# Gated linear attention on one core: the reference point of the log decays, one for each block of 128 tokens

## The chip, the cores and the metric

One core of a Trainium2 chip runs the whole kernel. The metric is the device time of one execution in microseconds (us), from repeated runs; the profile is one more execution, recorded instruction by instruction.

## The reference: what is computed

Two layers of an encoder on 256 tokens of 1024 channels, in float32. Each layer norms its input, projects it, feeds three mixers (a long convolution done as a Fourier product, a gated linear attention in both directions, a pooling mixer), merges them by gates, projects, and runs a gated MLP. The change is in the linear attention alone, which has 4 heads of 128 channels:

```python
def _gla_direction(q, k, v, log_a, include_diag):
    ...                                               # C = 64 tokens a chunk
    b = jnp.cumsum(log_a.reshape(B, N, C, H, DK), axis=2)
    b_last = b[:, :, -1]
    q_e = q * jnp.exp(b)
    k_e = k * jnp.exp(-b)
    scores = jnp.einsum('bnthd,bnshd->bnhts', q_e, k_e)
    ...                                               # triangular mask, product with v
    k_dec = k * jnp.exp(b_last[:, :, None] - b)
    U = jnp.einsum('bnshd,bnshe->bnhde', k_dec, v)
    decay = jnp.exp(b_last)
    ...                                               # state carried over the chunks
    o_inter = jnp.einsum('bnthd,bnhde->bnthe', q_e, S_prev)
```

Written out, a query at token t and a key at token s of one head meet with the factor exp(b_t - b_s), where b is the running sum of the log decays; the second direction runs from the last token to the first. Any common reference can be taken off both sums without changing the product.

## The kernel before

The 256 tokens are two blocks of 128. Almost all work is products of activations with weights that stream in from memory: SyncE loads a chunk of 128x2048, ScalarE (ACT, line 98) rounds it to a short float32 form, VectorE (DVE, line 103) subtracts to get the rest, and TensorE (PE, line 112, helper `mm`) multiplies three times for each pair (`mm3`: upper by upper, upper by lower, lower by upper). The main units (`two_ftiles`, `branch` and so on) are emitted one after the other; side work (`Side`, `start`, `tick`) is emitted between them a step at a time. Outside of stretches marked by `open_window` a list scheduler then sets the order on each engine; on the chip each engine takes its own list strictly in order. Tiles named `b` and `s` lie in SBUF (4096 and 2048 bytes a partition), `p` are the eight banks of PSUM.

The linear attention comes in three parts of a layer:

- `decay_gate(h)`, side work, four times: log decays of a head for both directions (z = 0, 1), two scans over the tokens (lines 663 and 665) which `rmask` restarts at each 64 tokens, then `e = exp(b)` and `en = exp(-b)`, each one ACTIVATE of 128x512, and two small copies (lines 672 and 673) of the exponentials at the chunk ends into `ebl`.
- `qk_post`: when queries and keys come from PE, they are multiplied into `eb` and `enb` (DVE line 106 for queries, 103 for keys).
- `gla_head(h)`, side work, four times: scores of a head, mask, product with `v`, norm, output gate, transposes. Since the sums restart every 64 tokens, a product over a block of 128 is right only inside each chunk of 64. The parts between two chunks are repaired: scaled copies of keys (`kx`) and queries (`q2`) are made by 6 ACTIVATEs and 6 DVE operations of 128x64, and for each block two matmuls of 64x64 (stationary 128x64, 64 moving columns) write over the wrong quarter of the block's scores:

```python
for t in range(2):
    for z in range(2):
        mm(pa[:, z, t, :], ke[:, z, s], qe[:, z, s], True, True)
    mm(pa[0:CH, 0, t, CH:], kx[:, 0, 0, cs(t)], qe[:, 0, cs(2 * t + 1)], True, True)
    mm(pa[CH:, 1, t, 0:CH], kx[:, 0, 1, cs(t)], qe[:, 1, cs(2 * t)], True, True)
```

These operands are plain float32, and each such matmul stands as two records in the trace (so 32 matmuls of 64x64 in the program are 64 records). Weight products run in the short form and are one record each.

Of the kernel before, what the change touches and what calls it, by code (L numbers as in the profile page):

```python
# [15 lines left out]
AF = mybir.ActivationFunctionType  # L16
ALU = mybir.AluOpType

P = 128
DEPTH = 2  # L20
L = 256
# [4 lines left out]
CH = 64  # L26
POOL_WINDOWS = (2, 4, 8, 16)
PAD = 8

# chunks of the weight stream, per layer  # L30
NCHUNK = 71

# columns of the packed per-channel vectors
V_HYC = 0            # 12 tiles x (w0, w1, w2, b)
V_FFC = 48           # 22 tiles x (w0, w1, w2, b)
V_GB = 136           # 2 dirs x 4 heads
V_PS = 148           # 4
V_FB = 152           # b1, fr1, b2, fr2 (64 rows, twice)
NVEC = 160
# [37 lines left out]
def trunk(ctx: ExitStack, tc: tile.TileContext, a: dict, out: bass.AP):  # L77
    nc = tc.nc
# [5 lines left out]
    sml = Slots(spool, "s", 9, 2048)  # L84
# [7 lines left out]
    ahead = {"chunks": 3, "reserve": 0, "at": 0, "quiet": False, "still": False}  # L92
# [4 lines left out]
    def act(o, i, func=AF.Copy, **kw):  # L97
        ins = nc.scalar.activation(o, i, func, **kw)  # L98
        if func in TABLED:
            tc.stamp_issue_order_token(ins.ins, TOKEN)  # L100
# [10 lines left out]
    def mm(o, w, x, start, stop):  # L111
        ins = nc.tensor.matmul(o, w, x, start=start, stop=stop).ins  # L112
        if not isinstance(ins, tuple):
            newest["pe"] = ins
# [12 lines left out]
    def open_window(*more):  # L127
        """From here on PE, DVE and ACT keep the order of emission; splits only where a chain leaves room."""
        e = mybir.EngineType
        window.enter_context(tc.manual_schedule(engines={e.PE, e.DVE, e.Activation, *more}))  # L130
        ahead["quiet"] = True
# [4 lines left out]

# [1 line left out]
    xs = [cpool.tile([P, DM], F32, name=f"x{t}") for t in range(2)]  # L138
# [5 lines left out]
    rmask = cpool.tile([P, L], F32, name="rmask")  # L144
# [18 lines left out]

# [1 line left out]
    order = []  # L165
# [56 lines left out]
    def split_half(lead=True):  # L222
        """One more half of a chunk is split; the upper parts run one half ahead."""
        if state["l"] >= 2 * len(order):
            return
        if state["h"] == state["l"]:
            split_upper()
        if lead and state["h"] == state["l"] + 1 and state["h"] // 2 in raws and len(big.free) >= ahead["reserve"] + 4:
            split_upper()
        split_lower()  # L230
# [5 lines left out]
    def weights(n, at, width):  # L236
        """Upper and lower part of columns of a chunk."""
        half, at = divmod(at, 1024)
        return wh[n][half][:, at:at + width], wl[n][half][:, at:at + width]
# [16 lines left out]
    def load_constants():  # L256
        nc.gpsimd.memset(rmask[:].rearrange("p (c s) -> p c s", s=CH)[:, :, 0:1], 0.0)
        nc.gpsimd.dma_start(zt[:], a["zt"])
        nc.gpsimd.dma_start(fw1[:], a["fw1"])
        nc.gpsimd.dma_start(fw2[:], a["fw2"])  # L260
        nc.gpsimd.dma_start(edges[:], bass.AP(a["edges"].tensor, a["edges"].offset, [[0, P], [1, 64]]))
        newest["pool"] = nc.gpsimd.dma_start(pmask_f[:], a["pmask"]).ins

# [1 line left out]
    sides = []  # L265
# [73 lines left out]

# [1 line left out]
    def rstd_of(ss, width, n=1):  # L341
# [22 lines left out]
    def rstd_mean(ss):  # L364
        """(mean + eps) ** -0.5 of a mean that lies in two parts."""
        r = cpool.tile([P, 1], F32, tag="rstd", bufs=4, name="rstd")
        e = cpool.tile([P, 1], F32, tag="mse", bufs=4, name="mse")
        tsc(e[:], ss[:, 0:1], ss[:, 1:2], EPS, ALU.add, ALU.add)
        nc.gpsimd.tensor_tensor(out=r[:], in0=e[:], in1=mhalf[:, 0:1], op=ALU.pow)  # L369
        return r  # L370
# [43 lines left out]

# [1 line left out]
    def filter_mlp(i, h2):  # L416
# [23 lines left out]

    # ---- the implicit filters, their spectra: even part on the cosines, odd part on the sines; even and odd times
    # apart, whose sum is the spectrum at f and whose difference that at 256 - f ----
    def load_dft(kf, n):
        """Upper and lower part; even or odd times; cosines, sines; 128 columns."""
        kf[n] = big.get([P, 2, 2, 2, P], F32R)
        with tc.issue_after(newest["pool"]):
            nc.gpsimd.dma_start(kf[n][:], a[n])
# [79 lines left out]

# [1 line left out]
    handles = {}  # L529
# [4 lines left out]
    def chunk_x_stationary(n, xt, t, o, half, lows_late=False):  # L534
        """Products of a chunk, 512 columns over half of the rows, with x stationary; lows_late takes lower parts last."""
        xth, xtl = xt[0][half], xt[1][half]
        s = slice(t * P, (t + 1) * P)
        todo = [(k, m) for k in range(4) for m in range(3)]
        if lows_late:
            todo.sort(key=lambda km: (km[0] // 2, (0, 2, 1)[km[1]]))  # L540
        for k, m in todo:
            h, l = weights(n, k * 512, 512)
            x = xtl if m == 2 else xth
            mm(o, x[:, k, s], l if m == 1 else h, half == 0 and (k, m) == todo[0], half == 1 and (k, m) == todo[-1])
# [22 lines left out]
    def layer(i, xt, chains):  # L567
# [8 lines left out]

        # -- value and output gate of the linear attention, token-major
        ahead.update(chunks=3, reserve=4)
# [12 lines left out]
        for at, (n, t) in enumerate(seq):  # L591
            drain(chains[t], alone=True)
            m, j = divmod(n, 2)
# [18 lines left out]

        # -- low rank of the decay gates: four groups of 32 rows, x w_h, x w_h, x w_l, x w_h, of which the first
        # two keep their upper part and the last its lower one; the second meets the lower part of the second factor
        nl = pos_of[("lr", i)]
# [22 lines left out]
        enb = [big.get([P, 2, 2, L]) for _ in range(2)]  # L638
        ebl = sml.get([P, 4, 2, 4])

# [6 lines left out]
        def decay_gate(h):  # L647
# [20 lines left out]
            yield  # L668
            act(e, en, AF.Exp)
            act(en, en, AF.Exp, scale=-1.0)  # L670
            ec = e.rearrange("p z (c s) -> p z c s", s=CH)
            nc.vector.tensor_copy(ebl[:, h, 0, :], ec[:, 0, :, CH - 1])
            nc.vector.tensor_copy(ebl[:, h, 1, :], ec[:, 1, :, 0])

# [13 lines left out]

        # -- Hyena: x1, v of the first and second half of the channels
        zv = big.get([P, 4, L])  # L690
# [132 lines left out]

        # -- queries and keys
        drain(f_dec, *gates_ready)
# [7 lines left out]

        # -- pooling
        pw = sml.get([P, 4, P])
# [69 lines left out]
        def gla_head(h):  # L905
            qe, ke = eb[h // 2][:, h % 2], enb[h // 2][:, h % 2]
            vh = slice(h * P, (h + 1) * P)
            cs = lambda c: slice(c * CH, (c + 1) * CH)
            e = lambda z, c: ebl[:, h, z, c:c + 1]
            kx = sml.get([P, 2, 2, P])  # L910
            q2 = sml.get([P, 2, P])
            sc = nc.vector.tensor_scalar_mul
            for z in range(2):
                for m in range(2):
                    act(kx[:, 0, z, cs(m)], ke[:, z, cs(2 * m + z)], scale=e(z, 2 * m + z))
            sc(kx[:, 1, 0, cs(0)], kx[:, 0, 0, cs(0)], e(0, 1))
            sc(kx[:, 1, 0, cs(1)], ke[:, 0, cs(1)], e(0, 1))
            sc(kx[:, 1, 1, cs(0)], ke[:, 1, cs(2)], e(1, 2))
            sc(kx[:, 1, 1, cs(1)], kx[:, 0, 1, cs(1)], e(1, 2))
            act(q2[:, 0, cs(0)], qe[:, 0, cs(2)])  # L920
            sc(q2[:, 0, cs(1)], qe[:, 0, cs(3)], e(0, 2))
            sc(q2[:, 1, cs(0)], qe[:, 1, cs(0)], e(1, 1))
            act(q2[:, 1, cs(1)], qe[:, 1, cs(1)])
            yield
# [3 lines left out]
            for t in range(2):  # L928
                s = slice(t * P, (t + 1) * P)
                for z in range(2):  # L930
                    mm(pa[:, z, t, :], ke[:, z, s], qe[:, z, s], True, True)
                mm(pa[0:CH, 0, t, CH:], kx[:, 0, 0, cs(t)], qe[:, 0, cs(2 * t + 1)], True, True)
                mm(pa[CH:, 1, t, 0:CH], kx[:, 0, 1, cs(t)], qe[:, 1, cs(2 * t)], True, True)
            for z in range(2):
                mm(pb[:, z, :], kx[:, 1, z, :], q2[:, z, :], True, True)
            yield
            sml.put(kx, q2)
            pm = sml.get([P, 4, P])
# [57 lines left out]

        # -- gates, branch projections, merge
        merged = []
# [61 lines left out]

        # -- output projection, post norm, residual, norm of the channel mixer
        ahead.update(chunks=6, reserve=2)
# [21 lines left out]

        # -- channel mixer
        NB = 4
# [184 lines left out]
def _constants():  # L1271
    """Arrays that depend on shapes alone."""
    t = np.linspace(0.0, 1.0, L, dtype=np.float32)[:, None]
# [130 lines left out]
```

## Time and profile before

| | |
|---|---|
| time of three runs, median (lowest to highest) | 907.86 us (907.23 to 908.74) |
| profiled execution, first to last instruction | 907.4 us |
| PE busy | 896.0 us, 99% of the span |
| PE weight loads busy | 836.9 us, 92% |
| DVE busy | 635.5 us, 70% |
| ACT busy | 500.2 us, 55% |
| GpSimd busy | 35.0 us, 4% |
| data moved | 164.61 MB, mean 181 GB/s |

The profiled execution has no time of its own beside its span; the median of the runs lies 0.46 us above that span. The ends of PE's records are modelled and successive records overlap, so what one matmul costs is read from the start of one row to the start of the next, not from its own duration.

### The profile page before, as it was taken

The numbers are of one execution on the slowest core, as the hardware profiler recorded it, in microseconds if no ns is written. First come the engines' busy times: TensorE is split into PE (matmuls) and PEld (weight loads), VectorE is DVE, ScalarE is ACT, GpSimd is POOL, SyncE is SP. The second block draws the span as 40 slices with busy tenths as digits, with TensorE's granted clock in tenths as the row PEclk, the third lists the DMA queues.
The fourth block names the chain that finished last, engine by engine and source line by source line (L and its number), as shares of the span: only waits on it lengthen the run. The fifth ranks groups of instructions, "written<-read, shape, count | busy, mean of one in ns | idle before, by whom it ended". The sixth has DMA issues, their size and how long they took to land.

```text
span 907.4 us, 15309 instructions
## 1 busy us (share of the span) xinstructions
PE 896.0 (99%) x6336; PEld 836.9 (92%) x6336; DVE 635.5 (70%) x934; ACT 500.2 (55%) x773; POOL 35.0 (4%) x80
## 2 busy tenths in 40 slices
PE   7999999999999999999999999999999999999997
PEld 6899999999988999998888999999999899999885
DVE  5899988666657798765288979775754967776612
ACT  6777656544446676545167744674542766554511
POOL 3000000100000000000010000000000000000000
PEclk9999999999999999999999999999999999999999
DMA  8863546446627436555439445264653583555601
GB/s 285 319 219 131 184 142 217 151 144 238 226 87 267 163 113 232 187 186 198 173 107 344 165 139 196 95 224 149 233 186 140 183 285 136 186 187 167 227 1 46
DMA packets 26020, 164.61 MB, mean 181 GB/s; under 512 B 3178, under 2 KB 3317, under 8 KB 8032
## 3 DMA queue, kind: packets, MB, share of 16 engines
q1 hardware_dynamic: 22464, 151.70, 47.2%
q0 software_dynamic: 3488, 11.95, 4.1%
q8 instruction: 49, 0.80, 0.3%
q14 instruction: 19, 0.16, 0.0%
HBM read 162.59 MB, written 1.05 MB: 180 GB/s over the span
## 4 chain that ended last, share of the span: by engine, by line
PE 97%; DMA 1%; DVE 1%; ACT 0%; issue 0%; SPq 0%; DVEq 0%; POOLq 0%; ACTq 0%
PE p L112 96%; DMA raw<-in_wts 1%; PE p L356 1%; PE p L1134 0%; DVE b L106 0%; DVE b L103 0%; PE p L738 0%; PE p L967 0%; ACT b L98 0%; SPq L151 0%; DVE x L106 0%; DVEq L1400 0%; ACT s L98 0%; POOLq L1400 0%; PE p L1217 0%
## 5 line engine op out<-in xcount | busy, mean ns | idle before, releaser
L112 PE MATMUL p<-b,b 128*128 128x256 f32 (+2 forms) x5958 | 858.4, 305 | 3.7 <-ACT b L98 2.4
L112 PEld LDWEIGHTS p<-b,b 128*128 128x128 f32 x5958 | 796.2, 191 | 54.1 <-ACT b L98 3.0
L103 DVE TENSOR_TENSOR b<-raw,b 128x1024 fp32r<-128x1024 f32 x286 | 343.0, 1217 | 126.0 <-ACT b L98 70.5
L98 ACT ACTIVATE b<-raw 128x1024 fp32r<-128x1024 f32 x288 | 290.8, 1045 | 196.5 <-PE p L112 163.6
L103 DVE TENSOR_TENSOR b<-p,b 128x512 f32<-128x512 f32 (+2 forms) x64 | 40.7, 653 | 59.8 <-ACT s L98 51.6
L98 ACT ACTIVATE b<-p 128x512 f32<-128x512 f32 (+3 forms) x78 | 43.5, 567 | 37.9 <-PE p L112 26.5
L98 ACT ACTIVATE s<-p 128x256 f32<-128x256 f32 (+3 forms) x50 | 20.3, 415 | 77.8 <-PE p L112 77.0
L106 DVE SCALAR_TENSOR_TENSOR s<-p,vec,s 128x255 f32<-128x255 f32 x104 | 49.4, 479 | 6.5 <-ACT s L98 5.5
L98 ACT ACTIVATE b<-b 128x512 f32<-128x512 f32 (+4 forms) x38 | 26.2, 692 | 24.1 <-DVE b L103 21.4
L98 ACT ACTIVATE s<-p,vec 128x256 f32<-128x256 f32 x52 | 28.7, 556 | 15.9 <-DVE s L106 13.0
L98 ACT ACTIVATE s<-s 128x512 f32<-128x512 f32 (+5 forms) x44 | 26.0, 594 | 14.2 <-DVE s L106 6.5
L103 DVE TENSOR_TENSOR b<-b,b 128x512 f32<-128x512 f32 (+4 forms) x34 | 26.6, 782 | 9.0 <-ACT b L98 8.6
L98 ACT ACTIVATE b<-s 128x512 fp32r<-128x512 f32 x38 | 23.6, 626 | 12.1 <-DVE s L103 12.0
L103 DVE TENSOR_TENSOR b<-s,b 128x512 fp32r<-128x512 f32 x38 | 25.9, 687 | 4.6 <-ACT b L98 4.6
L103 DVE TENSOR_TENSOR b<-b,p 128x512 f32<-128x512 f32 x24 | 16.4, 685 | 12.1 <-PE p L112 12.0
L112 PE MATMUL p<-b,s 128*64 128x64 f32 (+3 forms) x144 | 22.4, 286 | 0.0
L103 DVE TENSOR_TENSOR s<-s,p 128x512 f32<-128x512 f32 x22 | 15.0, 683 | 8.4 <-ACT s L98 8.0
L112 PEld LDWEIGHTS p<-b,s 128*128 128x128 f32 (+2 forms) x144 | 15.0, 166 | 5.7 <-issue 3.1
L106 DVE SCALAR_TENSOR_TENSOR b<-p,vec,b 128x255 f32<-128x255 f32 (+1 forms) x40 | 19.0, 480 | 1.7 <-ACT b L98 1.5
L103 DVE TENSOR_TENSOR s<-s,s 128x512 f32<-128x512 f32 (+2 forms) x24 | 15.7, 666 | 2.0 <-ACT s L98 2.0
L109 DVE TENSOR_SCALAR mse<-ssq 128x1 f32<-128x1 f32 (+1 forms) x24 | 4.7, 197 | 17.6 <-ACT s L98 13.7
L369 POOL TENSOR_TENSOR rstd<-mse,mhalf 128x1 f32<-128x1 f32 x16 | 8.8, 553 | 209.5 <-DVE mse L109 209.5
(96 smaller groups left out, 292.3 us busy)
## 6 DMA issues: line engine op xcount, KB each, us to landing
raw<-in_wts SPq DMA_DIRECT2D x140, 1024.0 KB, 4.9
b<-in_gains POOLq DMA_DIRECT2D x7, 512.0 KB, 6.7
raw<-in_wts SPq DMA_DIRECT2D x4, 512.0 KB, 8.1
b<-in_dft POOLq DMA_DIRECT2D x4, 512.0 KB, 5.3
x<-in_x SPq DMA_DIRECT2D x4, 256.0 KB, 4.8
b<-in_gw POOLq DMA_DIRECT2D x2, 512.0 KB, 5.6
b<-in_fw POOLq DMA_DIRECT2D x2, 512.0 KB, 6.4
b<-in_decay POOLq DMA_DIRECT2D x2, 512.0 KB, 7.4
```

The costliest lines, as they stand in the source:

```text
L98: ins = nc.scalar.activation(o, i, func, **kw)
L103: nc.vector.tensor_tensor(out=o, in0=x, in1=y, op=op)
L106: nc.vector.scalar_tensor_tensor(out=o, in0=x, scalar=s, in1=y, op0=op0, op1=op1)
L109: nc.vector.tensor_scalar(out=o, in0=x, scalar1=s1, scalar2=s2, op0=op0, op1=op1)
L112: ins = nc.tensor.matmul(o, w, x, start=start, stop=stop).ins
L356: nc.tensor.transpose(ps[k // 4][:, k % 4, :], h[:, k * P:(k + 1) * P], ident[:])
L369: nc.gpsimd.tensor_tensor(out=r[:], in0=e[:], in1=mhalf[:, 0:1], op=ALU.pow)
```

## The change

The scans restart every 128 tokens instead of every 64. Of the sum at each token the value at the middle of its block (token 63 of a block for the first direction, 64 for the second) is taken off inside the exponential, as a bias that differs by channel: so each 128x512 exponential becomes four of 128x128, one for each direction and block. The middle values and their negatives are two small DVE operations on four columns; two exponentials of the middle values and two of the block-end values are kept as the factors between the two blocks. With one reference for the whole block, the block's scores are right as they come from the 128x128 matmul; the 64x64 matmuls and the scaled copies for them are gone, and only the product between the blocks keeps scaled copies (`kq`), two ACTIVATEs and two DVE operations of 128x128 a head.

```diff
-        nc.gpsimd.memset(rmask[:].rearrange("p (c s) -> p c s", s=CH)[:, :, 0:1], 0.0)
+        nc.gpsimd.memset(rmask[:].rearrange("p (c s) -> p c s", s=P)[:, :, 0:1], 0.0)
...
-        ebl = sml.get([P, 4, 2, 4])
+        ebl = sml.get([P, 4, 3, 4])
...
-            act(e, en, AF.Exp)
-            act(en, en, AF.Exp, scale=-1.0)
-            ec = e.rearrange("p z (c s) -> p z c s", s=CH)
-            nc.vector.tensor_copy(ebl[:, h, 0, :], ec[:, 0, :, CH - 1])
-            nc.vector.tensor_copy(ebl[:, h, 1, :], ec[:, 1, :, 0])
+            at = lambda ap, o, *dims: bass.AP(ap.tensor, ap.offset + o, [list(ap.ap[0]), *map(list, dims)])
+            mid, neg, cross = (ebl[:, h, j, :] for j in range(3))
+            nc.vector.tensor_copy(at(mid, 0, (2, 2), (1, 2)), at(en, CH - 1, (L + 1, 2), (P, 2)))
+            nc.vector.tensor_scalar_mul(neg, mid, -1.0)
+            for z in range(2):
+                for b in range(2):
+                    s = slice(b * P, (b + 1) * P)
+                    act(e[:, z, s], en[:, z, s], AF.Exp, bias=neg[:, 2 * z + b:2 * z + b + 1])
+            for z in range(2):
+                for b in range(2):
+                    s = slice(b * P, (b + 1) * P)
+                    act(en[:, z, s], en[:, z, s], AF.Exp, scale=-1.0, bias=mid[:, 2 * z + b:2 * z + b + 1])
+            act(cross[:, 2:4], mid[:, 1:3], AF.Exp)
+            nc.vector.tensor_copy(cross[:, 0:2], at(e, P - 1, (L + 1, 2)))
...
-            kx = sml.get([P, 2, 2, P])
-            q2 = sml.get([P, 2, P])
-            sc = nc.vector.tensor_scalar_mul
+            kq = sml.get([P, 2, 2, P])
             for z in range(2):
-                for m in range(2):
-                    act(kx[:, 0, z, cs(m)], ke[:, z, cs(2 * m + z)], scale=e(z, 2 * m + z))
-            sc(kx[:, 1, 0, cs(0)], kx[:, 0, 0, cs(0)], e(0, 1))
-            sc(kx[:, 1, 0, cs(1)], ke[:, 0, cs(1)], e(0, 1))
-            sc(kx[:, 1, 1, cs(0)], ke[:, 1, cs(2)], e(1, 2))
-            sc(kx[:, 1, 1, cs(1)], kx[:, 0, 1, cs(1)], e(1, 2))
-            act(q2[:, 0, cs(0)], qe[:, 0, cs(2)])
-            sc(q2[:, 0, cs(1)], qe[:, 0, cs(3)], e(0, 2))
-            sc(q2[:, 1, cs(0)], qe[:, 1, cs(0)], e(1, 1))
-            act(q2[:, 1, cs(1)], qe[:, 1, cs(1)])
+                cross = lambda j: ebl[:, h, 2, 2 * j + z:2 * j + z + 1]
+                act(kq[:, 0, z, :], ke[:, z, z * P:(z + 1) * P], scale=cross(0))
+                nc.vector.tensor_scalar_mul(kq[:, 1, z, :], qe[:, z, (1 - z) * P:(2 - z) * P], cross(1))
...
-                mm(pa[0:CH, 0, t, CH:], kx[:, 0, 0, cs(t)], qe[:, 0, cs(2 * t + 1)], True, True)
-                mm(pa[CH:, 1, t, 0:CH], kx[:, 0, 1, cs(t)], qe[:, 1, cs(2 * t)], True, True)
             for z in range(2):
-                mm(pb[:, z, :], kx[:, 1, z, :], q2[:, z, :], True, True)
+                mm(pb[:, z, :], kq[:, 0, z, :], kq[:, 1, z, :], True, True)
```

PE's list at the fourth head of the first layer, before: `p_72` are the scores inside the blocks, `p_73` those between the blocks, `p_69` and `p_74` units of the gates with weights `b_147` to `b_150`.

```order
L112 MATMUL p_69_2062<-b_2_104,b_148_1830 128x256
L112 MATMUL p_72_2154<-b_48_435,b_50_437 128x128 x2
L112 MATMUL p_72_2154<-b_48_435,s_50_2096 64x64 x2
L112 MATMUL p_72_2154<-b_48_435,b_50_437 128x128 x2
L112 MATMUL p_72_2154<-b_48_435,s_50_2096 64x64 x2
L112 MATMUL p_73_2155<-s_51_2097,s_50_2096 128x128 x2
L112 MATMUL p_74_2166<-b_1_103,b_149_1877 128x256
```

The same place in the list of the changed kernel.

```order
L112 MATMUL p_69_2055<-b_2_104,b_148_1840 128x256
L112 MATMUL p_69_2055<-b_2_104,b_147_1839 128x256
L112 MATMUL p_69_2055<-b_4_106,b_147_1839 128x256
L112 MATMUL p_72_2138<-b_48_435,b_50_437 128x128 x4
L112 MATMUL p_73_2139<-s_47_2089 128x128 x2
L112 MATMUL p_74_2146<-b_1_103,b_149_1883 128x256
```

The four matmuls of 64x64 are gone and the six of 128x128 stand in one row; nothing has come in their place.

ACT's list at the decay gate of the first head in the first layer, before: `b_47` takes the exponential and `b_49` its inverse, `s_12`, `s_10` feed the filter spectra by `b_31`, `b_33`, `s_14` is the gate of the next head.

```order
L98 ACTIVATE s_14_730<-s_14_730 128x512
L98 ACTIVATE b_47_434<-b_49_436 128x512
L98 ACTIVATE s_19_824<-p_24_690,vec 128x256
L98 ACTIVATE b_31_323<-s_12_662 128x512
L98 ACTIVATE b_49_436<-b_49_436 128x512
L98 ACTIVATE b_33_325<-s_10_660 128x512
L98 ACTIVATE b_78_892<-raw_688 128x1024
```

The same place of the changed kernel; `s_7` holds the middle values.

```order
L98 ACTIVATE s_14_730<-s_14_730 128x512
L98 ACTIVATE s_19_832<-p_24_690,vec 128x256
L98 ACTIVATE b_31_323<-s_12_662 128x512
L98 ACTIVATE b_47_434<-b_49_436,s_7_438 128x128 x4
L98 ACTIVATE b_49_436<-b_49_436,s_7_438 128x128 x3
L98 ACTIVATE b_33_325<-s_10_660 128x512
L98 ACTIVATE b_49_436<-b_49_436,s_7_438 128x128
L98 ACTIVATE s_7_438<-s_7_438 128x2
L98 ACTIVATE b_78_916<-raw_688 128x1024
```

The first exponential has moved behind the work for `s_19` and `b_31`, and seven of the eight small exponentials now stand ahead of the split `b_33` that had one of 128x512 ahead of it.

## Rows read from the trace of the kernel before

**Rows 1.** The page: span, and busy time of each engine.

```profile
span 907.4 us, 15309 instructions
PE 896.0 (99%) x6336; PEld 836.9 (92%) x6336; DVE 635.5 (70%) x934; ACT 500.2 (55%) x773; POOL 35.0 (4%) x80
```

**Rows 2.** Waits of PE over the whole span: total us, times, longest.

```profile
PE p L112 <- ACT b L98: 2.4, 1, 2.4
PE p L112 <- DVE b L103: 1.3, 2, 1.1
```

**Rows 3.** Busy time by stretch: length, PE, PEld, DVE, ACT, POOL; clock, DMA.

```profile
0.00:20.00 20.00, 15.25 (x67) 12.72 (x67) 8.67 (x22) 11.43 (x28) 7.06 (x21) 0.91 0.87 278
...
60.00:100.00 40.00, 40.00 (x302) 37.18 (x301) 39.09 (x73) 30.23 (x51) 1.64 (x3) 1.00 0.43 153
...
163.00:200.00 37.00, 37.00 (x314) 36.00 (x311) 22.39 (x40) 17.48 (x41) 2.65 (x4) 1.00 0.37 134
```

**Rows 4.** Groups of PE by shape: all matmuls of 64x64.

```profile
L112 PE MATMUL p<-b,s 128*64 128x64 f32 x64 | 7.0, 246 | 0.0
```

**Rows 5.** PE in order of time at the fourth head: start, us, form.

```profile
180.53 0.34 PE L112 MATMUL p<-b,s 128*64 128x64 f32 x4
180.79 0.71 PE L112 MATMUL p<-b,b 128*128 128x128 f32 x4
181.43 0.34 PE L112 MATMUL p<-b,s 128*64 128x64 f32 x4
```

**Rows 6.** The same stretch in cuts of 10 ns, so single records stand apart.

```profile
180.10 0.39 PE L112 MATMUL p<-b,b 128*128 128x128 f32 x2
...
180.32 0.28 PE L112 MATMUL p<-b,b 128*128 128x128 f32 x1
...
181.01 0.39 PE L112 MATMUL p<-b,b 128*128 128x128 f32 x2
```

**Rows 7.** PE in order of time, score-by-value products of the third head.

```profile
176.22 1.06 PE L112 MATMUL p<-b,s 128*128 128x128 f32 x8
177.03 0.36 PE L112 MATMUL p<-b,b 128*128 128x256 f32 x1
```

**Rows 8.** PE in order of time, first 64x64 matmul of the program.

```profile
140.22 0.33 PE L112 MATMUL p<-b,s 128*64 128x64 f32 x2
140.48 0.62 PE L112 MATMUL p<-b,b 128*128 128x256 f32 x3
```

**Rows 9.** PE in order of time, last 64x64 matmuls of the program.

```profile
621.78 0.34 PE L112 MATMUL p<-b,s 128*64 128x64 f32 x4
```

**Rows 10.** Groups of ACT by shape.

```profile
L98 ACT ACTIVATE b<-b 128x512 f32<-128x512 f32 x16 | 9.9, 623 | 0.2
...
L98 ACT ACTIVATE s<-b,s 128x64 f32<-128x64 f32 x32 | 8.3, 337 | 0.5 <-DVE s L103 0.5
...
L98 ACT ACTIVATE b<-p,gcol 128x128 fp32r<-128x128 f32 x16 | 4.5, 389 | 2.6 <-PE p L1217 2.6
L98 ACT ACTIVATE s<-p 128x128 f32<-128x128 f32 x16 | 4.3, 276 | 3.0 <-PE p L112 3.0
```

**Rows 11.** Groups of DVE: one of six scalings, one of two copies.

```profile
L916 DVE TENSOR_SCALAR s<-s,s 128x64 f32<-128x64 f32 x8 | 2.0, 251 | 0.0
...
L673 DVE COPY s<-b 128x4 f32<-128x4 f32 x8 | 1.3, 168 | 0.0
```

**Rows 12.** ACT and DVE in order of time, decay gates of the first layer.

```profile
79.45 0.61 ACT L98 ACTIVATE b<-b 128x512 f32<-128x512 f32 x1
79.96 0.62 ACT L98 ACTIVATE b<-s 128x512 fp32r<-128x512 f32 x1
...
98.70 1.30 ACT L98 ACTIVATE b<-b 128x512 f32<-128x512 f32 x2
...
104.28 1.29 DVE L106 SCALAR_TENSOR_TENSOR b<-p,b 128x512 f32<-128x512 f32 x2
```

**Rows 13.** PE in order of time: the spectrum matmuls behind that split.

```profile
80.69 1.19 PE L112 MATMUL p<-b,b 128*128 128x512 f32 x7
```

More of the change, by code (lines that the diff above doesn't have):

```diff
@@ L907, in gla_head @@
             vh = slice(h * P, (h + 1) * P)
-            cs = lambda c: slice(c * CH, (c + 1) * CH)
-            e = lambda z, c: ebl[:, h, z, c:c + 1]
-            kx = sml.get([P, 2, 2, P])
-            q2 = sml.get([P, 2, P])
-            sc = nc.vector.tensor_scalar_mul
-            for z in range(2):
-                for m in range(2):
-                    act(kx[:, 0, z, cs(m)], ke[:, z, cs(2 * m + z)], scale=e(z, 2 * m + z))
-            sc(kx[:, 1, 0, cs(0)], kx[:, 0, 0, cs(0)], e(0, 1))
-            sc(kx[:, 1, 0, cs(1)], ke[:, 0, cs(1)], e(0, 1))
-            sc(kx[:, 1, 1, cs(0)], ke[:, 1, cs(2)], e(1, 2))
-            sc(kx[:, 1, 1, cs(1)], kx[:, 0, 1, cs(1)], e(1, 2))
-            act(q2[:, 0, cs(0)], qe[:, 0, cs(2)])
-            sc(q2[:, 0, cs(1)], qe[:, 0, cs(3)], e(0, 2))
-            sc(q2[:, 1, cs(0)], qe[:, 1, cs(0)], e(1, 1))
-            act(q2[:, 1, cs(1)], qe[:, 1, cs(1)])
+            kq = sml.get([P, 2, 2, P])
+            for z in range(2):
+                cross = lambda j: ebl[:, h, 2, 2 * j + z:2 * j + z + 1]
+                act(kq[:, 0, z, :], ke[:, z, z * P:(z + 1) * P], scale=cross(0))
+                nc.vector.tensor_scalar_mul(kq[:, 1, z, :], qe[:, z, (1 - z) * P:(2 - z) * P], cross(1))
             yield
@@ L931, in gla_head @@
                     mm(pa[:, z, t, :], ke[:, z, s], qe[:, z, s], True, True)
-                mm(pa[0:CH, 0, t, CH:], kx[:, 0, 0, cs(t)], qe[:, 0, cs(2 * t + 1)], True, True)
-                mm(pa[CH:, 1, t, 0:CH], kx[:, 0, 1, cs(t)], qe[:, 1, cs(2 * t)], True, True)
             for z in range(2):
-                mm(pb[:, z, :], kx[:, 1, z, :], q2[:, z, :], True, True)
+                mm(pb[:, z, :], kq[:, 0, z, :], kq[:, 1, z, :], True, True)
             yield
-            sml.put(kx, q2)
+            sml.put(kq)
             pm = sml.get([P, 4, P])
```

## Prediction

> **What bounds the kernel now.** I read the page first: PE is busy 896.0 of 907.4 us [rows 1]. A busy PE can still hide waits, so the waits come next: PE waited for ACT once, 2.4 us, and for DVE twice, 1.3 us in all [rows 2]. The table by stretch puts these at the start: the first 20 us hold 15.25 us of PE work, while both stretches of the middle that matter here, 60 to 100 and 163 to 200 us, are full to the last hundredth, at the granted clock of 1.00, that is at the 2.4 GHz level [rows 3]. So from 20 us on the end of the kernel is set by the sum of PE's intervals. Work taken off PE's list comes off the time one for one, as long as no other engine becomes late; work added to ACT or DVE costs nothing, as long as PE's operands and banks come in time.
>
> **What is removed on PE.** 32 matmuls of 64x64 go, 64 records with 7.0 us of busy time [rows 4]. That column isn't their price, since successive records overlap and the neighbours may be held up too. The price is read from starts. At the fourth head four records of 64x64 start at 180.53 and the next row at 180.79: 0.26 us for the group itself [rows 5]. The neighbours: 128x128 records ahead of the group start at 180.10 (two of them) and 180.32, so 0.22 / 2 = 0.11 us each; but from the last of them, 180.32, to the first 64x64 record at 180.53 it is 0.21 [rows 5, 6]. Behind the group the first 128x128 record starts at 180.79 and the second at 181.01: 0.22 instead of 0.11 [rows 5, 6]. So each side of a group costs 0.10 to 0.11 us more than a plain interval. One group is 0.26 + 0.10 + 0.10 = 0.46 us.
>
> Is the side cost really that of the 64x64 shape, not of these float32 products standing amid the short-form stream? The eight records of 128x128 at 176.22 are float32 too, follow other work and are followed by the stream at 177.03: 0.81 us for eight, 0.10 each, no side cost at either end [rows 7]. So it is the shape.
>
> Here a rule bears on how to count. The Trainium skill, TensorEngine Tiling (Array Packing), sections Key Properties and Theoretical Speedup, says that parts of 64 columns can run side by side, for up to twice the speed, and that a change of tiling mode drains TensorE. By its first half alone the removed matmuls would be cheap, down to half of their busy time, 3.5 us in all as an estimate; by its second half each group pays for entering and leaving. The trace agrees with both: it shows the sharing inside a group and the price at its sides.
>
> From rows, the sharing looks like this: the first group of the program has two records only, and from 140.22 to the next row at 140.48 it is 0.26 us as well, the same as for four [rows 8]. So the price goes by groups and not by matmuls. In the trace of the whole program I count 21 groups, 12 in the first layer and 9 in the second, of which 11 have four records and 10 have two (11 x 4 + 10 x 2 = 64), the first at 140.22 and the last at 621.78 [rows 8, 9]. 21 x 0.46 = 9.7 us. Rounding of the starts leaves about 0.01 us per group, so 9.4 to 10.0. Between the lists nothing takes their place on PE: the six 128x128 matmuls of a head are unchanged in number and shape, and in the list of the fourth head they stand together. The filter spectra move by some tens of rows in the first layer, with nothing added. The lists of SyncE and GpSimd keep their rows but for a memset of two columns instead of four, so no transfer moves past another; `gla_head` holds one `s` tile where it held two.
>
> **What is added and removed on ACT.** Per head, two exponentials of 128x512 at 623 ns go and eight of 128x128 come. The trace has no such operation from SBUF with a bias by channel; the nearest are 389 ns (a per-channel scale, from PSUM) and 276 ns (no per-channel operand) [rows 10]. So 2.2 to 3.1 us instead of 1.25, plus one tiny exponential, which I bound by 0 and 0.28. I take the upper end, since the 389 ns row also has a per-channel operand: at most +2.1 us per head, +1.0 at least. In `gla_head` six ACTIVATEs of 128x64 go, of which the four with a scale alone are 1.35 us (337 ns each; the two plain copies I leave out), and two of 128x128 come, 0.55 to 0.78 us: at least -0.6 to -0.8 us [rows 10]. Over the 8 heads of both layers ACT's total moves by +2 to +12 us on 500; it isn't near the bound as a whole. What counts is the stage of the decay gates.
>
> **What is added and removed on DVE.** Per head, two copies of four columns (168 ns) become two copies and one small product: +0.17 us; six scalings of 128x64 (251 ns, 1.5 us) become two of 128x128, which I bound by 0.25 and 0.50 each (one and two of the old): -0.5 to -1.0 us [rows 11]. DVE as a whole gets lighter, but the +0.17 us falls into 60 to 100 us, where it is busy 39.09 of 40 [rows 3].
>
> **The cover of the decay stage.** The longer chain of a head is: scan, copy, negative, four exponentials, four more. With the prices above it is 0.17 + 0.17 + 3.1 - 1.25 = 2.2 us longer than before. Who waits for it: the queries' product on DVE (line 106), behind which DVE's list and, through the PSUM bank it frees, PE's. In the first layer the last two exponentials start at 98.70 and are done at 100.00; the first query product starts at 104.28 [rows 12]. That leaves 4.3 us, more than the 2.2 us of one chain. If all four heads' extra ACT work ran up without being absorbed, it would be 4 x 2.1 = 8.4 us, against 40 - 30.23 = 9.8 us of idle ACT in the stretch [rows 3]: it just fits, so I cost it at nothing. If that cover is gone, the query products are late by 8.4 - 4.3 = 4.1 us.
>
> **Sum.** 907.4 - 9.7 = 897.7 us of span. The median of the runs shown is 0.46 us above the profiled span, so 898.2 us: 1.1% faster.
>
> **The rivals.**
>
> *The 64x64 work runs beside other work, and only part of its price comes back.* Then the sides stay, for instance since a float32 block has such an edge wherever the list puts it, and 21 x 0.26 = 5.5 us come off: 902.4 us. For it: groups of two and of four cost the same, so something does run side by side; and the list around the heads is rebuilt, so that other neighbours meet. Against it: the plain edges of the eight 128x128 records. Chance 0.06. It is the first half of the page's rule, that parts of 64 columns share the array, which would lead here.
>
> *The decay stage becomes late by part of its cover.* PE then waits up to 4.1 us in the first layer for banks or for spectra, and the time is 898.2 + 1.5 to 4.1, that is 899.7 to 902.3. For it: DVE has 0.9 us free in 40, and ACT would go from 30.23 to as much as 38.6. Against it: the same crowding costs PE nothing now. Chance 0.11.
>
> *Each head's exponentials hold up a split that PE needs at once.* This is the one on the other side. On ACT the split into `b_33` used to have one 128x512 exponential ahead of it and has seven of 128x128 in the new list. Such a split can be just in time: the one into `b_31` at 79.96 stands right behind an exponential (79.45) and ends at 80.58, and the spectrum matmuls that read it start at 80.69 [rows 12, 13]. If PE stood still for the extra work of every one of the 8 heads, at 1.0 to 2.1 us, that is 8 to 17 us, against 9.7 gained: it decides from 1.2 us per head, and at 2.1 the time would be 898.2 + 16.8 = 915. Against it: PE has gone through 8 such heads with no wait on record, because the list gives it weight products in between, and the first exponential was moved behind such a split. Chance 0.05; about 0.04 of no change lies between, with a wait of some 9 to 11 us.
>
> What I forecast has the rest, 0.74.
>
> **How the numbers follow.** A measurement of this kernel can tell about 0.2% from no change, 1.8 us. The forecast's own span is 9.4 to 10.0 us gained with up to 1.5 us lost to new waits, or a little more gained if the rebuilt list also drops some short stalls: 896.6 to 899.8. To leave out no more than 2 in 10 the range reaches on to 901.5, which takes in most of the second rival. Faster: 0.74 + 0.06 + 0.11 = 0.91; same 0.04; slower 0.05.
>
> **What would show each step right or wrong.** Right: the group of 64x64 matmuls is missing; in PE's order of time no interval of 0.2 us stands at a 128x128 record beside another shape in the heads; PE's busy time is near 896.0 - 9.7 = 886.3; PE's waits still sum to under 5 us, all at the start. The first rival would show as 0.2 us edges at the 128x128 runs. The second as waits of PE, or starved stretches of PE, between 60 and 140 us, with the query products of line 106 later relative to PE's work. The third as a new row of PE waiting for ACT, around the spectra. My prediction is wrong if PE's busy time falls by 9.7 but its idle time grows, since then the lists, and not the work, set the end; or if the starts that I read as a price were waits for scaled copies that something else would have filled.

## The result, and the profile after

| | before | after |
|---|---|---|
| median of four runs each, taken together (lowest to highest) | 907.56 us (907.23 to 908.74) | 901.64 us (900.64 to 902.33) |
| ratio, with 95% interval | | 0.9931 (0.9919 to 0.9943) |

The kernel is faster by 5.2 to 7.4 us, where 9.7 were forecast. The median is 0.14 us above the upper end of my range, inside the times of the second rival (899.7 to 902.3).

The page of the changed kernel, against [rows 1]:

```profile
span 898.9 us, 15183 instructions
PE 886.0 (99%) x6272; PEld 830.5 (92%) x6272; DVE 630.9 (70%) x910; ACT 505.8 (56%) x797; POOL 35.0 (4%) x80
```

PE is busy 886.0 us, where 886.3 were forecast. A part of that agreement is luck: the profiled run of before had the slower start (granted clock 0.91 in its first 20 us [rows 3], 1.00 here). Of the 10.0 us by which PE's busy time fell, 0.8 lie ahead of its 201st record, where both kernels have the same work; from there on it falls from 855.7 to 846.5 us, by 9.2. The waits of PE are the next thing to look at, against [rows 2]. Columns: total us, times, longest.

```profile
PE p L112 <- DVE b L103: 3.5, 3, 2.2
PE p L112 <- ACT b L98: 1.4, 1, 1.4
PE p L112 <- DVE rmask L246: 1.2, 1, 1.2
PE p L112 <- DMA b<-in_il: 0.5, 1, 0.5
```

Two of these are new: one of 2.2 us for DVE's line 103 and one of 0.5 us for a DMA. The wait for `rmask`, a mask made at the start, stands in both kernels; [rows 2] leave it out. The table by stretch says where; columns as in [rows 3].

```profile
0.00:20.00 20.00, 16.13 (x74) 13.04 (x74) 10.63 (x26) 13.38 (x31) 7.06 (x21) 1.00 0.86 281
60.00:100.00 40.00, 40.00 (x308) 38.03 (x308) 37.92 (x75) 31.39 (x66) 1.60 (x3) 1.00 0.33 119
100.00:140.00 40.00, 39.53 (x320) 38.85 (x320) 33.94 (x56) 24.11 (x41) 2.13 (x9) 1.00 0.48 164
140.00:163.00 23.00, 20.84 (x176) 20.64 (x175) 20.99 (x35) 15.14 (x28) 0.72 (x1) 1.00 0.69 236
```

The stretch with the decay gates, 60 to 100 us, is still full. PE stands still 0.47 us between 100 and 140 and 2.16 us between 140 and 163, at a granted clock of 1.00. The chain of waits leads back from the second hole (start, us, what):

```profile
113.49 9.00 DMA b<-in_il
...
122.54 13.96 PE p L112 x114
...
143.21 0.61 DVE b L103
```

PE's last link is the inverse transform of the convolution. All links from its end at 136.5 us to 143.82 are DVE's, one operation behind the other. DVE in order of time shows what it did there (the first row, a query product, is read further down):

```profile
106.70 0.68 DVE L106 SCALAR_TENSOR_TENSOR b<-p,b 128x512 f32<-128x512 f32 x1
...
137.23 0.68 DVE L103 TENSOR_TENSOR b<-p,b 128x512 f32<-128x512 f32 x1
...
139.06 0.47 DVE L923 TENSOR_SCALAR s<-b,s 128x128 f32<-128x128 f32 x2
139.45 2.35 DVE L103 TENSOR_TENSOR b<-raw,b 128x1024 fp32r<-128x1024 f32 x2
141.72 0.70 DVE L103 TENSOR_TENSOR b<-b 128x532 f32<-128x532 f32 x1
...
143.13 0.68 DVE L103 TENSOR_TENSOR b<-b,b 128x512 fp32r<-128x512 f32 x1
```

At 137.23 the second half of the convolution's output is multiplied (in `hyena`, `tt(zv...)`). Its lower split, which PE waits for, starts at 143.13. In between DVE works without a gap, on two splits of weights, on pooling steps, on the new scalings `kq` (line 923) and on a few more. That is 5.9 us from the multiplication to the split, but it isn't new. DVE at the same place before:

```profile
134.83 0.68 DVE L103 TENSOR_TENSOR b<-p,b 128x512 f32<-128x512 f32 x1
...
137.31 2.35 DVE L103 TENSOR_TENSOR b<-raw,b 128x1024 fp32r<-128x1024 f32 x2
...
140.92 0.69 DVE L103 TENSOR_TENSOR b<-b,b 128x512 fp32r<-128x512 f32 x1
```

There it took 6.1 us, with the same two splits of weights in between, and PE had no wait. PE in order of time has both holes of the changed kernel (the last three rows, the fourth head, are read further down):

```profile
122.54 14.42 PE L112 MATMUL p<-b,b 128*128 128x256 f32 x118 [0.47 <-DMA b<-in_il]
136.80 0.88 PE L112 MATMUL p<-s,s 128*128 128x256 f32 x6
137.52 2.61 PE L112 MATMUL p<-b,b 128*128 128x256 f32 x21
...
143.86 2.41 PE L112 MATMUL p<-b,b 128*128 128x256 f32 x18 [2.16 <-DVE b L103]
...
176.77 0.94 PE L112 MATMUL p<-b,b 128*128 128x128 f32 x7
177.55 0.61 PE L112 MATMUL p<-s 128*128 128x128 f32 x4
177.91 6.00 PE L112 MATMUL p<-b,b 128*128 128x256 f32 x48
```

PE goes on at 143.86, 0.73 us behind the start of that split. And PE before:

```profile
134.40 0.88 PE L112 MATMUL p<-s,s 128*128 128x256 f32 x6
135.12 5.17 PE L112 MATMUL p<-b,b 128*128 128x256 f32 x42
```

The six records of a pooling product (`p<-s,s`) start in both kernels 0.43 us ahead of DVE's multiplication. Before, 42 records and then the heads' follow them and cover DVE's stretch; now it is 21, and then 14 more up to the hole. The other work is not gone: the first of the six is PE's 899th record before and its 929th now, so 30 more records stand ahead of it.

Why does the output stand so late in PE's list? ACT in order of time, in the changed kernel (the first row, the last exponentials of the fourth head, is for later):

```profile
104.87 0.68 ACT L98 ACTIVATE b<-b,s 128x128 f32<-128x128 f32 x2
...
123.30 0.61 ACT L98 ACTIVATE b<-s 128x512 fp32r<-128x512 f32 x1
123.93 1.28 ACT L98 ACT_TABLE_LOAD   x1
126.32 1.06 ACT L98 ACTIVATE b<-b 128x1024 f32<-128x1024 f32 x1 [1.10 <-PE p L112]
127.28 0.58 ACT L98 ACTIVATE b<-p 128x512 f32<-128x512 f32 x1
127.76 0.62 ACT L98 ACTIVATE b<-s 128x512 fp32r<-128x512 f32 x1
```

And the same place before:

```profile
122.60 1.14 ACT L98 ACTIVATE b<-s 128x512 fp32r<-128x512 f32 x2
123.75 1.28 ACT L98 ACT_TABLE_LOAD   x1
```

Before, both last splits of the convolution's spectrum (`b<-s`, 128x512) stood ahead of the table load for the gate's sigmoid. In the changed kernel only one does; the other stands behind the load, the sigmoid (which itself waits for PE) and a copy, and starts 4.46 us after the first. The theory which the experiments had to test: the inverse transform's operands come late by this list, so the scheduler puts other work of PE ahead of its end, and too little is left behind it to cover the 6 us that DVE takes. PE never stands still for the late split itself: it has no wait near 128 us, where the split runs. The hole at 122.54 lies ahead of the split in time, and this theory doesn't account for it.

Runs of one kernel differ by up to 4 us, the longer ones mostly at a lower mean granted clock (in one kernel below 897.87 us at 0.999 and 900.90 at 0.994), so the fastest runs stand beside the medians.

### The profile page after: what moved, and what is told of

Its sections match the earlier page's. It is cut to its first block, busy times and chain, and to the rows that moved or that the text cites. A ratio compares the mean times of both kernels' runs of the same rounds, so it can differ in the third digit from the quotient of the medians.

```text
span 898.9 us, 15183 instructions
## 1 busy us (share of the span) xinstructions
PE 886.0 (99%) x6272; PEld 830.5 (92%) x6272; DVE 630.9 (70%) x910; ACT 505.8 (56%) x797; POOL 35.0 (4%) x80
## 4 chain that ended last, share of the span: by engine, by line
PE 96%; DMA 2%; DVE 2%; issue 0%; ACT 0%; SPq 0%; DVEq 0%; POOLq 0%; ACTq 0%
PE p L112 94%; DMA b<-in_il 1%; DVE b L103 1%; DMA raw<-in_wts 1%; PE p L356 1%; PE p L1132 0%; DVE b L106 0%; PE p L749 0%; PE p L965 0%; ACT b L98 0%; SPq L151 0%; DVE s L923 0%; DVE x L106 0%; DVEq L1398 0%; ACT s L98 0%
## 5 line engine op out<-in xcount | busy, mean ns | idle before, releaser
L98 ACT ACTIVATE s<-s 128x512 f32<-128x512 f32 (+6 forms) x52 | 27.7, 532 | 13.4 <-DVE s L106 8.2
L98 ACT ACTIVATE b<-b 128x512 fp32r<-128x512 f32 (+3 forms) x22 | 16.3, 742 | 24.8 <-DVE b L103 23.6
L98 ACT ACTIVATE b<-b,s 128x128 f32<-128x128 f32 x64 | 20.5, 391 | 1.0 <-DVE s L674 0.9
L112 PE MATMUL p<-b,s 128*128 128x128 f32 (+1 forms) x80 | 15.7, 315 | 0.0
```

## The experiments

The first four kernels ran together, with 17 runs of the kernel before: median 907.68 us, fastest 906.50. The last three ran together with 11 runs of it: median 906.68, fastest 906.32. The changed kernel was timed apart from both, with the four runs of before in the first table; against the kernel before of its own round each, it gained 5.9 us by the medians and 6.6 by the fastest runs.

The last column leaves the start out. It is read from the traces: the time from the start of PE's 201st record (at 42.6 to 46.0 us; all kernels have the same records up to there) to the end of PE's last one. Before it is 855.7 us, and in the changed kernel 849.1: 6.6 us less.

| kernel | median us | fastest | ratio to before (95%) | PE from its 201st record, us |
|---|---|---|---|---|
| before without 64x64 matmuls | 897.37 | 896.99 | 0.9891 (0.9873 to 0.9908) | 846.0 |
| before with eight exponentials a head | 908.08 | 906.27 | 0.9996 (0.9984 to 1.0008) | 855.1 |
| before, 64x64 matmuls grouped | 904.50 | 903.00 | 0.9960 (0.9945 to 0.9975) | 852.3 |
| after, sigmoid behind the split | 900.18 | 898.48 | 0.9912 (0.9897 to 0.9927) | 847.4 |
| after with two exponentials | 897.76 | 897.29 | 0.9894 (0.9877 to 0.9911) | 846.4 |
| before with the new heads | 898.32 | 897.23 | 0.9897 (0.9879 to 0.9914) | 846.3 |
| after, two edits of order | 899.15 | 897.87 | 0.9906 (0.9890 to 0.9923) | 846.7 |

**The price of the 64x64 matmuls, alone.** The kernel before without them; all scaled copies are still made.

```diff
-                mm(pa[0:CH, 0, t, CH:], kx[:, 0, 0, cs(t)], qe[:, 0, cs(2 * t + 1)], True, True)
-                mm(pa[CH:, 1, t, 0:CH], kx[:, 0, 1, cs(t)], qe[:, 1, cs(2 * t)], True, True)
```

> The kernel before, with the 32 matmuls of 64x64 left out and nothing else changed (the scaled copies are still made; the scores between the two 64-token chunks of a block are not repaired, so the output is not the reference's). Theory: the price of the 64x64 groups is 0.46 us each and all of it is on the path, so 9.7 us come off the time before (907.6): 897.9, and the wait of about 2.3 us that the changed kernel has near 141 us is missing, because ACT's list keeps the last spectral split ahead of the table load. Rival 1: the side costs stay or the matmuls partly ran beside other work: 5.5 us or less come off, 902.1 or more. Rival 2: the 64x64 matmuls were filling a wait for the second half of the convolution's output, so without them PE waits there whatever ACT's list: about 901.6, as the changed kernel.

Measured: 10.3 us less by the medians, 9.5 by the fastest runs and 9.7 by the last column, against the 9.7 of the sum. On the page PE is busy 885.2 us. All waits of PE:

```profile
PE p L112 <- ACT b L98: 1.4, 1, 1.4
PE p L112 <- DVE rmask L246: 1.2, 1, 1.2
PE p L112 <- DVE b L103: 1.2, 1, 1.2
```

All these waits lie in the first 20 us. So the price was right, it lay on the path in full, and the 64x64 matmuls had not been filling a wait.

**Does the price go by groups?** The kernel before with the four 64x64 matmuls of a head written behind its six of 128x128, which leaves 11 groups instead of 21.

```diff
             for z in range(2):
                 mm(pb[:, z, :], kx[:, 1, z, :], q2[:, z, :], True, True)
+            for t in range(2):
+                mm(pa[0:CH, 0, t, CH:], kx[:, 0, 0, cs(t)], qe[:, 0, cs(2 * t + 1)], True, True)
+                mm(pa[CH:, 1, t, 0:CH], kx[:, 0, 1, cs(t)], qe[:, 1, cs(2 * t)], True, True)
```

> The kernel before, with a head's four 64x64 matmuls written after its six of 128x128, so that PE's list has 11 groups of them instead of 21 (five of four, three of three, three of one). Theory of a price by groups: entering and leaving cost 0.20 us a group and the groups' own time is 0.26 us for up to two matmuls and 0.52 for three or four, so 3 x 0.46 + 8 x 0.72 = 7.1 instead of 9.7 us: about 2.5 us less than before (905.1). Rival, a price by matmul: no change.

Measured: 3.2 us less by the medians, 3.5 by the fastest runs, 3.4 by the last column, for the same 64 records. The interval of the times, 2.3 to 5.0 us, would hold my expectation of 2.5 as well as 4.6 for ten groups at 0.46. The trace decides. One group of four matmuls:

```profile
176.81 0.45 PE L112 MATMUL p<-b,s 128*64 128x64 f32 x8
177.19 0.98 PE L112 MATMUL p<-b,b 128*128 128x256 f32 x6
```

It takes 0.38 us from start to start, where I had expected 0.52; one or two matmuls take 0.26. The 11 groups of the trace (five of four matmuls, of which one takes 0.65, three of three at 0.38, three of one) sum to 4.1 us, and with 0.20 us at the sides of each to 6.3, against 9.7: 3.4 us less, as measured. So most of the price goes by groups, and a larger group costs a little more.

**The longer exponentials, alone.** The kernel before with eight exponentials of 128x128 a head, whose bias is a column of zeros.

```diff
-            act(e, en, AF.Exp)
+            for z in range(2):
+                for b in range(2):
+                    s = slice(b * P, (b + 1) * P)
+                    act(e[:, z, s], en[:, z, s], AF.Exp, bias=zero[:, 2 * z + b:2 * z + b + 1])
```

(The inverse likewise.)

> The kernel before, with the two exponentials of a head of 128x512 split into eight of 128x128 with a bias column of zeros; the 64x64 matmuls stay. Theory: the longer exponentials are covered, so the time stays within 1 us of the time before (907.6), with no new wait of PE. Rival: the crowded stage of the decay gates alone makes the filter's spectra or the convolution late, and it costs 2 to 4 us: 909.6 to 911.6.

Measured: no difference. Their group:

```profile
L98 ACT ACTIVATE b<-b,zero 128x128 f32<-128x128 f32 x64 | 20.8, 394 | 0.0
```

One costs 394 ns, and the crowded stage covers it. ACT's list at the convolution has, as before, both spectral splits ahead of the table load (120.64 and 121.79 us).

**The sigmoid held back.** The changed kernel; the gate's sigmoid may issue on ACT only behind the last spectral split.

```diff
-                split(yh[b][:, 1, :], yl[b][:, 1, :], p2[:])
+                newest["hy"] = nc.scalar.activation(yh[b][:, 1, :], p2[:], AF.Copy).ins
+                tt(yl[b][:, 1, :], p2[:], f32(yh[b][:, 1, :]), ALU.subtract)
...
+            with tc.issue_after(newest["hy"]):
-            act(gt[:], sg[:], AF.Sigmoid)
+                act(gt[:], sg[:], AF.Sigmoid)
```

> The changed kernel, with the sigmoid of the output gate in ACT's list held behind the last spectral split of the convolution, so that this split no longer waits for the table load, the sigmoid of 128x1024 and a bank copy. Theory: this misplaced split made the inverse transform late and PE used up its other work early; with it in place the wait near 141 us (2.3 us) goes, and with luck the one at 122 us (0.6 us): 898.7 to 899.3 against 901.6 of the changed kernel. Rival: the lateness comes from the crowded VectorE or from the late landing of the inverse transform's matrix, so that PE still waits about 2 us near there: 901 to 902.

Measured: 900.18 us, above what I expected. Against the kernel before of its round it gains 7.5 us (8.0 by the fastest runs), where the changed kernel gained 5.9 (6.6). The intervals of the two ratios overlap, so the times alone don't tell the two kernels apart; by the last column the edit gives back 1.7 us (849.1 to 847.4). PE in order of time, around both holes:

```profile
123.71 13.21 PE L112 MATMUL p<-b,b 128*128 128x256 f32 x108 [0.35 <-DMA b<-in_il]
...
137.48 3.80 PE L112 MATMUL p<-b,b 128*128 128x256 f32 x31
...
143.44 2.78 PE L112 MATMUL p<-b,b 128*128 128x256 f32 x21 [0.58 <-DVE b L103]
```

The wait for DVE falls from 2.16 to 0.58 us: the place of that one split caused most of it. PE's list shows how: ten of the records that stood ahead of the pooling product are back behind it (31 instead of 21, and 108 instead of 118 ahead). The wait for `in_il` stays, so this split didn't cause it.

**DVE's order as well.** The kernel above, with DVE's splits of weight chunks held behind the second split of the convolution's output.

```diff
+            with tc.issue_after(newest["hy2"]) if "hy2" in newest else ExitStack():
-            tt(wl[n][half][:], raws[n][:, half * 1024:(half + 1) * 1024], f32(wh[n][half][:]), ALU.subtract)
+                tt(wl[n][half][:], raws[n][:, half * 1024:(half + 1) * 1024], f32(wh[n][half][:]), ALU.subtract)
```

(`hy2` is the lower split of the second half in `hyena`.)

> The changed kernel with two edits of order: the gate's sigmoid on ACT is held behind the last spectral split, and DVE's lower splits of weight chunks are held behind the lower split of the convolution's second half. Theory (what is left of the wait near 142 us is DVE taking two lower splits of weights first): the 0.74 us wait near 142.6 goes, only 0.5 us for the inverse transform's second matrix stays: 898.6 to 899.6 us. Rival (the wait left is for ACT's upper split, so DVE's order doesn't matter): 900.2 again. A third way: the held weight splits are late for their own products near 148 us, 901 or more.

Measured: 899.15 us, as expected; a gain of 7.5 us by the medians, no more than the kernel above, 8.5 by the fastest runs, and 0.8 us less than the kernel above by the last column. The weight splits still ran in time for their own products. PE's first hole, and the stretch of the second (columns as in [rows 3]), in which PE is now full:

```profile
125.18 13.21 PE L112 MATMUL p<-b,b 128*128 128x256 f32 x108 [0.44 <-DMA b<-in_il]
...
140.00:163.00 23.00, 23.00 (x196) 23.00 (x195) 21.11 (x32) 15.14 (x31) 0.00 (x0) 1.00 0.60 213
```

This is the best version with the reference's output: its only wait left beyond the start, of those that the change brought, is that for `in_il`.

**Which part of the change reordered the list?** First the changed kernel with the two old exponentials instead of the eight, the rest of the gate kept.

```diff
-            for z in range(2):
-                for b in range(2):
-                    s = slice(b * P, (b + 1) * P)
-                    act(e[:, z, s], en[:, z, s], AF.Exp, bias=neg[:, 2 * z + b:2 * z + b + 1])
+            act(e, en, AF.Exp)
...
+            act(en, en, AF.Exp, scale=-1.0)
```

> The changed kernel, but each head has its two plain exponentials of 128x512 instead of eight small ones with a bias; the middle values, their negatives and the two tiny exponentials stay. The decay factors are then not taken from the block's middle, so the output isn't the reference's. ACT's list has the second spectral split ahead of the gate's table load again. Theory (the longer gate chain reordered ACT's list in the first layer, and that made the convolution's output late): PE waits under 1 us behind 20 us, time 897.4 to 899.0 us. Rival 1 (the wait comes from the new scalings kq of the heads on DVE, whatever the gate does): the wait of some 2 us near 141 us stays, 900.5 to 901.6. Rival 2 (the eight exponentials themselves hold ACT too long): also 897.4 to 898, but then the wait near 141 us is gone without the spectral split having moved.

Then the kernel before with the heads' part of the change alone.

```diff
-            kx = sml.get([P, 2, 2, P])
-            q2 = sml.get([P, 2, P])
...
+            kq = sml.get([P, 2, 2, P])
+            for z in range(2):
+                act(kq[:, 0, z, :], ke[:, z, z * P:(z + 1) * P], scale=e(z, 1))
+                nc.vector.tensor_scalar_mul(kq[:, 1, z, :], qe[:, z, (1 - z) * P:(2 - z) * P], e(z, 2))
```

> The kernel before with the heads' part of the change alone: two ACTIVATEs and two DVE scalings of 128x128 a head instead of the scaled copies of 128x64, no matmuls of 64x64; the sums still restart every 64 tokens and the exponentials are the old ones, so the scores between two chunks of 64 tokens of a block are left unrepaired. Theory (the price of the 64x64 groups comes back in full as long as the gate's part stays as it was): no wait of PE behind 20 us, 907.7 - 9.7 to 10.2 = 897.5 to 898.0 us. Rival (the heads' part reorders the lists or is late on DVE): a wait of PE near 141 us, 899.5 to 901.6.

Measured: 897.76 and 898.32 us, fastest 897.29 and 897.23. Against the kernel before of their round they gain 8.9 and 8.4 us (9.0 and 9.1 by the fastest runs); by the last column they stand 0.4 and 0.3 us above the kernel without the 64x64 matmuls. ACT in order of time, of the changed kernel with two exponentials:

```profile
122.90 1.14 ACT L98 ACTIVATE b<-s 128x512 fp32r<-128x512 f32 x2
124.06 1.28 ACT L98 ACT_TABLE_LOAD   x1
```

Both splits are ahead of the table load again, and neither kernel shows a wait of PE between 20 and 500 us. So the new heads alone cost 0.4 us at most. The eight exponentials are needed for the loss, but it isn't their own time: in the kernel before they left ACT's list at this place, and the time, as they were. Only together with something else of the change do they make the list scheduler place the split behind the table load: the two small DVE operations ahead of them, the new heads, or both. No run here separates these.

## Why the prediction was right, and where it failed

**What bounds the kernel: right.** Where the 64x64 matmuls went and the split kept its place, in three kernels, the time fell by 8.4 to 10.3 us (9.3 to 9.7 by the last column).

**The price of the removed work: right.** 9.7 us were forecast and 9.7 came off by the last column when these matmuls alone went. The edges are gone with them: at the fourth head of the changed kernel, against [rows 5, 6], seven records take from 176.77 to 177.55 and four from there to 177.91 (PE's rows above), 0.11 and 0.09 us each, with no 0.2 at either end. This rules out the first rival, although its 902.4 us is near the result.

**Durations on ACT and DVE: right, at the upper end where I took it.** ACT's groups, and one of DVE, against [rows 10, 11]:

```profile
L98 ACT ACTIVATE b<-b,s 128x128 f32<-128x128 f32 x64 | 20.5, 391 | 1.0 <-DVE s L674 0.9
...
L98 ACT ACTIVATE s<-b,s 128x128 f32<-128x128 f32 x16 | 5.5, 393 | 0.5 <-DVE s L103 0.5
L923 DVE TENSOR_SCALAR s<-b,s 128x128 f32<-128x128 f32 x16 | 3.8, 280 | 0.0
```

**The cover of the decay stage: right for the stage.** The last exponentials of the fourth head start at 104.87 and take 0.68, and the next query product starts at 106.70 (ACT's and DVE's rows above), so the 4.3 us shrank to about 1.2; but PE is full from 60 to 100 us, and its one wait between 100 and 140 is that for `in_il`, not for banks or query products.

**The step that failed: "The filter spectra move by some tens of rows in the first layer, with nothing added".** I read the moved rows of the lists only for work added to PE, and costed the reordering at nothing. But engines that follow strict lists pay for an order too. One split of 0.62 us was placed behind a table load and a sigmoid, 30 records of PE moved ahead of the end of the inverse transform, and PE waited 2.16 us behind it. Counted from start to start, beyond the usual interval of such a record, it is 2.3 us. The edit that put the split back returned ten of the 30 records and took 1.6 us off this wait; the one of DVE's order took the rest. What moved the other 20 ahead was not tested.

**The same step, at the transfers: "so no transfer moves past another".** Each queue kept its own rows, but the two queues shifted against each other, and PE waited 0.47 us for `in_il`, 0.6 from start to start. The issues in the changed kernel:

```profile
112.06 0.53 POOL L804 DMA_DIRECT2D b<-in_ih  x1 [23.89 <-PE p L112]
...
113.27 0.33 SPq L185 DMA_DIRECT2D raw<-in_wts  x1
```

And before:

```profile
113.26 0.33 SPq L185 DMA_DIRECT2D raw<-in_wts  x1
...
114.22 0.53 POOL L793 DMA_DIRECT2D b<-in_ih  x1 [20.13 <-ACT b L98]
```

A chunk of weights of 1024 KB that was issued ahead of both halves of the inverse transform's matrix now goes out between them, 0.22 us ahead of `in_il` (113.49 in the chain above). Both landed 9.0 us after their issue; before, the chunk took 4.9 and `in_il` 5.6.

Together the two waits are 2.3 + 0.6 = 2.9 us, and 9.7 - 2.9 = 6.8 us, inside the measured 5.2 to 7.4; the last column has 6.6. The time and the place, behind the gate stage of the first layer, are those of the second rival (1.5 to 4.1 us), but not its mechanism: the crowded stage alone cost nothing (the run with eight exponentials), and PE waited for the convolution's output and a transfer, not for query products. Its chance of 0.11 was too low even so, since the lists that I had read already stood in another order.

**A smaller step that failed: the 0.46 us between span and time.** I set the profiled span of before against the median of other executions. Executions of the changed kernel lie 1.7 to 1.8 us above their own spans, and the profiled one of before had a slower start (granted clock 0.91 in its first 20 us [rows 3], 1.00 in that of after). The forecast is not hurt, since it came off a median in effect; but the 8.5 us between the two profiled spans are for that reason not the gain. And the 899.8 us up to which I let the forecast's own span reach is 900.0 by its own terms (907.86 - 9.4 + 1.5), which doesn't move the forecast or the range.

**What stays open.** The wait for `in_il` remained under both edits of order. In these two and in the changed kernel the chunk of weights is issued between `in_ih` and `in_il`, and `in_il` takes 8.9 to 9.0 us; in the other six kernels the chunk is issued first, and it takes 4.9 to 6.2. So the shared loading is the likely reason, but no run moves that one transfer alone, and none shows why the chunk is issued at another place. Nor did I test which of the scheduler's estimates tips the split over.

## What to carry to other kernels

Where PE is the bound, price small matmuls from start to start, with their neighbours' edges, and by groups; that price came back in full here wherever the lists kept their order. Then read the reordered lists of the other engines at the next place where a chain of transforms feeds PE, not only where the edit stands: a split that lands behind a table load or behind an operation that waits for PE delays everything that hangs on it, and what counted here is how much of PE's work the list left behind as cover. Of 3.1 us lost against the kernel without the 64x64 matmuls, a pin of one instruction's place gave back 1.7, and one more 0.8. Where the start of a run varies, compare traces from a record behind it.

## What the runs showed of the hardware

A group of 64x64 float32 matmuls amid 128-wide ones costs 0.10 us at each side besides its own time, which is 0.26 us for one or two matmuls and 0.38 for three or four (one group of four took 0.65). The 512 KB of `in_il` in the first layer landed 4.9 to 6.2 us after their issue in six kernels, and 8.9 to 9.0 in the three where a transfer of 1024 KB was issued 0.2 us ahead of them.

In the nine profiled runs the granted clock of the first 20 us was 1.00, 0.91 or 0.83, with a mean over the whole run of 0.998 to 0.999, 0.996 to 0.997 and 0.994 to 0.995 in that order; after 20 us it was 1.00, the 2.4 GHz level, in all stretches read. One run of the kernel with eight exponentials has a mean of 0.945 at 908.98 us; its trace wasn't kept, so where its clock was low stays open.
